# Hybrid encoder layer on one core: cross-attention scores of passes two to four from seven of eight block products, with the weights' block sums made in two side jobs

## The chip, the cores and the metric

The kernel runs on one core of a Trainium2 chip. Five engines matter here, and each works through its own list of instructions strictly in order: PE (matrix products, with its weight loads shown apart as PEld), DVE (vector work), ACT (scalar work and activations), POOL (small vector work, and the issuing of some DMAs), SP (the issuing of most DMAs). The metric is the device time of one execution in microseconds. Below, q0 to q3 are the four groups of 512 tokens in the setup's linears, and "pass 0 to 3" are the four passes of the later stage over the same groups; the title's "passes two to four" are passes 1, 2 and 3 by their number in the code.

## The reference, cut to what matters

```python
h = x + concat(dilated_attention(q, k, v), conformer_conv(a, g)) @ w_out   # q, k, v, a, g = rmsnorm(x) @ w_in
xq = (rmsnorm(h) @ w_xq).reshape(B, S, 4, 256)
xk = (rmsnorm(mem) @ w_xk).reshape(B, 256, 4, 256)
xv = (rmsnorm(mem) @ w_xv).reshape(B, 256, 4, 256)
sc = einsum('bshd,bmhd->bhsm', xq, xk) * 256 ** -0.5
h = h + (einsum('bhsm,bmhd->bshd', softmax(sc), xv)).reshape(B, S, D) @ w_xo
h = h + square(relu(rmsnorm(h) @ w_up)) @ w_down
return rmsnorm(h)                                   # S = 2048 tokens, D = 1024, w_up to 4096
```

## The kernel before

**Arithmetic.** Every fp32 product is made of three fp16 products, high by high, high by low and low by high (`mm3`, L374 to L376). A weight tile is loaded as fp32 and split into its high part by ACT (L361) and its low part by DVE (L362).

**The setup** (to about 500 us) folds the memory's keys into the scratch array `ascr`, so that the cross-attention's scores are one product of the token columns with a 1024 x 512 matrix for each of two pairs of heads, and its values into `bscr`. Then it makes the linears q, k, the conv's gate and input (`glu`: unit g, then unit a, for each of four column groups) and v, over all 2048 tokens. The raw weights of q lie in the slots q0 to q3 of the pool `wqk` (tiles `qksq`), those of k in q4 to q7. The part around 400 us runs: the last q tile (512 tokens by all of q's weights), the gate unit g3 (weights `ws_g30`), the input unit a3 (weights `ws_a30`), then v (`wv0`, `wv1`). Woven in between are the weights' bounds (`scan`: loads on SP, sums of squares into `sjunk` on ACT), the first token group's convolution (`conv0`, DVE), and `vscale`: for each of four column groups it squares the v weights (`vsq`, ACT, L760 on), sums them by eight thin matmuls into `vss` (PE, L767), and brings the square root's power of two by DVE and POOL to `vbc` (PE, L355), by which DVE scales the raw v weights (L798); ACT rounds them to `wv` (L800), POOL makes the low part (L801).

**The passes.** `post(p)` handles 512 tokens: the out projection (`resid_linear`, "o"; it leaves the residual `h` and, by ACT and DVE, the token columns `yh` and `yl` for the next product, L1531 and L1532), the scores (`xs`, L1772 to L1790), the softmax and its transposes, the product with `bscr` ("x"), and the MLP (up and down). While a pass runs, `weave` puts in the next pass's attention (`att`), its convolution (`conv`) and the sums of `prep`, so many steps of each to one of the pass.

**The scores before** are for each pass two pairs of heads x 8 groups of 128 columns of D x 4 groups of 128 tokens x 3 = 192 matmuls of 128x512. The weights come from `ascr` in four fp32 tiles a pair, split on ACT and DVE (`wpost`).

**Seven of eight.** Part of the MLP's up products are made already with seven instead of eight block products (`quad`, L1660 to L1714). Its weights' block sums are made by `prep` (L1536 to L1605) in earlier passes and stored to the scratch array `ust`, seven tiles of 512 KB for each group; its token columns come from `put_columns` (L1623 to L1649), which writes sums such as `T1`, `T4`, `B2`, `T32` instead of `yh` and `yl`. `prep` makes a group in two halves: two loads `pw0`, `pw1`, then four sums (`ps`, in place in `pw`) and four tiles `pt0` to `pt3`, each a high part by ACT and a low part by DVE, and a store of each.

**What sets the order.** A scheduler fixes each engine's list when the kernel is built, from the program's order, the steps that `weave` mixes and the constraints of `pinned` and `after`. A tile in a pool's slot waits for the last reader of the tile that had the slot before.

Of the kernel before, what the change touches and what calls it, by code (L numbers as in the profile page):

```python
# [10 lines left out]
F32 = mybir.dt.float32  # L11
# [10 lines left out]
P = 128  # L22
# [26 lines left out]
def hybrid_layer(ctx, tc, A, out):  # L49
# [70 lines left out]
    ust = [[dr.tile([P, 2 * 1024], F16, name=f"ust{fg}_{i}") for i in range(7)] for fg in range(8)]  # L120
# [26 lines left out]
    gxm = cst.tile([P, 24], F32, name="gxm")  # L147
# [5 lines left out]
    cst.tile([P, 56], F32, name="cpad")  # L153
# [101 lines left out]
    def bounds():  # L255
# [9 lines left out]
        with ExitStack() as st:  # L265
# [15 lines left out]
            TS(c[18], c[18], 16.0, None, op0=ALU.mult)  # L281
# [11 lines left out]
        with ExitStack() as st:  # L293
# [14 lines left out]
            TS(gxm[:, 16:24], gxm[:, 8:16], -1.0, None, op0=ALU.mult)  # L308
        yield
# [153 lines left out]


# [542 lines left out]
    vsc = vscale()  # L1007
    scn = pinned(chain(scan(), bounds()), "pe", "act")
    with ExitStack() as st:
        cu = pool("conv0", stack=st)  # L1010
        conv0 = pinned(conv_units(cu, 0, ahead=False), "dve")
        with ExitStack() as st2:
            lbk = pool("lin_k", stack=st2)
            weave(islice(steps, 2), (vsc, 0.4))
            weave(islice(steps, 32), (vsc, 0.4), (conv0, 0.78), (scn, 1.6))
            drain(vsc)
            next(steps)
        lbv = pool("lin_v", stack=st)
        weave(islice(steps, 3), (scn, 2))
        weave(islice(steps, 5), (conv0, 1.05), (scn, 2))  # L1020
# [3 lines left out]
        weave(steps, (conv0, 1.05), (scn, 2))  # L1024
        drain(conv0, scn)
# [347 lines left out]
    def flat(t):  # L1373
        return t.rearrange("p h a b -> p (h a b)")

# [133 lines left out]
    def resid_linear(load, rhs, korder, resid, hs, ssum, scale, gains, y, name, steps=False, wide=False, put=None):  # L1509
# [26 lines left out]
    def prep(fgs, q):  # L1536

        late = []

        def give(d, t):  # L1540
            late.append((d, t))

        def step():
            for d, t in late:
                dma(d, t, q)
            late.clear()

        def hi(o, i):
            ACT.activation(o, i, AF.Copy, scale=S_UP)

        def lo(o, i, h):
            DVE.scalar_tensor_tensor(o, i, S_UP, h, op0=ALU.mult, op1=ALU.subtract)

        for fg in fgs:
            for j in range(2):
                nm = f"{fg}{j}"
                raw = [ct0.tile([P, 8, P], F32, tag=f"ch{i}", name=f"pw{i}_{nm}") for i in range(2)]
                step()
                for i in range(2):
                    dma(raw[i], wcols(w_up, (4 * fg + 2 * i + j) * P), q)  # L1560
# [46 lines left out]
    def columns(p):  # L1607

        names = {"B11": 0, "T1": 1, "T4": 2}
        if p == 1:  # L1610
            names["B12"] = 7
# [567 lines left out]
```

## Time and profile before

| | |
|---|---|
| times of three runs (us) | 2649.49, 2649.41, 2641.41; median 2649.41 |
| the profiled execution's own time (us) | 2644.86 |
| its span in the profile (us) | 2643.0 |
| busy: PE, DVE, ACT, POOL | 2588.1 (98%), 1947.6 (74%), 1239.1 (47%), 307.3 (12%) us |
| score stages of passes 1, 2 and 3 (us from the span's start) | 1235.2 to 1290.6, 1747.0 to 1795.5, 2237.1 to 2281.3 |
| last q tile's matmuls end | 386.5 us |
| `ws_g30`'s last matmul starts; first v matmul | 397.0 us; 409.8 us |

Times in the profile are microseconds from the span's start unless marked ns. A row of groups by line gives line, engine, operation, output <- inputs, sizes and count, then busy time, mean ns of one, the idle time just before them and what ended most of it. A row of one tile gives shortest/mean/longest ns, then when the first and last began. A row of the timeline gives start, duration, engine, line, operation. In rows of windows the columns are the window, its length, each engine's busy time with its count of instructions, the granted clock of PE, the share of time that the DMA engines were busy, and GB/s.

### The profile page before, as it was taken

Reading aid. Unit: us, or ns where it says so; the run is one execution under the profiler, and the core shown is the slowest. Engines: PE = TensorE matmul, PEld = TensorE weight load, DVE = VectorE, ACT = ScalarE, POOL = GpSimd, SP = SyncE. Lnnn points to the kernel's source line nnn. Section 1 sums busy time; section 2 is a strip of 40 time slices with the busy share of each in tenths; the row PEclk is TensorE's granted clock in tenths of the full one; section 3 lists DMA queues with packets and bytes.
Section 4 is the critical chain, followed back from the end, with each engine's and each line's share of the span. In section 5 each row is a group of like instructions: output and inputs, shape, how many; then the busy total and the mean of one; then the engine's idle time right before and its main releaser. Section 6 shows DMA issues by size and latency. Waiting matters only on the chain.

```text
span 2643.0 us, 45573 instructions
## 1 busy us (share of the span) xinstructions
PE 2588.1 (98%) x17710; PEld 1650.8 (62%) x17710; DVE 1947.6 (74%) x3775; ACT 1239.1 (47%) x2194; POOL 307.3 (12%) x417
## 2 busy tenths in 40 slices
PE   8999999999999999999999999999999999999998
PEld 7844448777455555545576676555776664468886
DVE  5887756567667999775799986467899557675666
ACT  5737645376454345544553344255443234452323
POOL 1134101132100110110001111000110000000000
PEclk9999999999999999999999999999999999999999
DMA  8987977766634657785367677454686465345442
GB/s 263 300 266 221 284 233 258 194 177 189 186 98 139 193 175 244 219 271 162 108 213 218 200 240 238 165 162 132 216 264 192 145 203 167 100 133 170 156 138 78
DMA packets 401753, 509.51 MB, mean 193 GB/s; under 512 B 81181, under 2 KB 295121, under 8 KB 400768
## 3 DMA queue, kind: packets, MB, share of 16 engines
q1 hardware_dynamic: 380816, 446.35, 55.3%
q0 software_dynamic: 15536, 51.24, 6.0%
q10 hardware_dynamic: 5184, 9.01, 0.9%
q8 instruction: 139, 2.28, 0.4%
q14 instruction: 78, 0.64, 0.1%
HBM read 390.75 MB, written 115.75 MB: 192 GB/s over the span
## 4 chain that ended last, share of the span: by engine, by line
PE 77%; DVE 12%; DMA 6%; issue 2%; ACT 2%; SPq 0%; POOL 0%; DVEq 0%; POOLq 0%; ACTq 0%
PE dn L375 7%; PE dn L376 7%; PE dn L374 7%; PE up L376 6%; PE up L375 6%; PE up L374 6%; PE lin L376 3%; PE lin L374 3%; PE lin L375 3%; DVE cacc L391 3%; PE xs L375 2%; PE xs L376 2%; PE xs L374 2%; PE pt L1047 2%; PE o L374 2%
## 5 line engine op out<-in xcount | busy, mean ns | idle before, releaser
L391 DVE SCALAR_TENSOR_TENSOR cacc<-cu,cw,cacc 128x512 f32<-128x512 f32 x480 | 364.4, 765 | 5.5
L375 PE MATMUL dn<-hhl,ws_d 128*128 128x512 f16 x768 | 290.6, 379 | 1.4 <-DVE hhl L1878 0.8
L374 PE MATMUL dn<-hhh,ws_d 128*128 128x512 f16 x768 | 287.9, 379 | 3.7 <-ACT hhh L1655 2.3
L376 PE MATMUL dn<-hhh,ws_d 128*128 128x512 f16 x768 | 290.5, 379 | 0.0
L1040 DVE CUSTOM_DVE_ANT_0 sm<-s,mask,qks 128x256 f32<-128x256 f32 (+1 forms) x384 | 151.1, 433 | 31.6 <-PE s L1081 28.0
L1041 ACT ACTIVATE sm<-sm,o 128x256 f32<-128x256 f32 (+1 forms) x288 | 119.3, 455 | 110.9 <-DVE o L1040 110.3
L1051 DVE TENSOR_TENSOR pl<-pt,ph 128x512 f16<-128x512 f32 x160 | 109.7, 685 | 42.1 <-ACT ph L1050 41.7
L374 PEld LDWEIGHTS <-ws_t 128*128 128x128 f16 x1232 | 120.6, 98 | 18.2 <-DMA ws_t<-ust 1.8
L376 PEld LDWEIGHTS <-ws_d 128*128 128x128 f16 x768 | 75.1, 98 | 90.4 <-issue 2.0
L375 PEld LDWEIGHTS <-ws_t 128*128 128x128 f16 x1232 | 120.5, 98 | 17.5 <-issue 2.3
L1050 ACT CAST ph<-pt 128x512 f16<-128x512 f32 x160 | 91.4, 571 | 84.5 <-PE pt L1047 84.3
L376 PEld LDWEIGHTS <-ws_t 128*128 128x128 f16 x1232 | 120.5, 98 | 16.8 <-issue 1.1
L374 PEld LDWEIGHTS <-ws_d 128*128 128x128 f16 x768 | 75.1, 98 | 84.7 <-issue 2.5
L375 PEld LDWEIGHTS <-ws_d 128*128 128x128 f16 x768 | 75.4, 98 | 83.7 <-issue 1.6
L1904 DVE SCALAR_TENSOR_TENSOR h<-dn,bd,h 128x512 f32<-128x512 f32 x96 | 71.5, 746 | 74.0 <-PE dn L376 73.7
L1047 PE MATMUL pt<-ident,sm 128*128 128x128 f32 x640 | 98.2, 274 | 4.6 <-ACT sm L1041 2.9
L374 PE MATMUL up<-mh,ws_u 128*128 128x512 f16 x256 | 98.1, 383 | 2.1 <-DVE rl L1875 2.1
L1687 ACT ACTIVATE e<-e 128x512 f32<-128x512 f32 x88 | 55.2, 629 | 95.3 <-DVE e L1685 95.3
L376 PE MATMUL up<-mh,ws_u 128*128 128x512 f16 x256 | 98.1, 384 | 1.3 <-DVE ws_u L362 1.3
L375 PE MATMUL up<-ml,ws_u 128*128 128x512 f16 x256 | 98.1, 383 | 0.0
L374 PE MATMUL up<-T32h,ws_t 128*128 128x256 f16 x352 | 95.9, 273 | 2.1 <-DMA ws_t<-ust 2.1
L374 PE MATMUL o<-cath,ws_o 128*128 128x512 f16 x256 | 96.5, 379 | 0.9 <-ACT cath L1219 0.8
(560 smaller groups left out, 7751.3 us busy)
## 6 DMA issues: line engine op xcount, KB each, us to landing
ws_t<-ust SPq DMA_DIRECT2D x154, 512.0 KB
ws_d<-wst SPq DMA_DIRECT2D x80, 512.0 KB
ust<-pt POOLq DMA_DIRECT2D x36, 512.0 KB, 5.1
scan<-in_w_up_dram SPq DMA_DIRECT2D x32, 512.0 KB
scan<-in_w_down_dram SPq DMA_DIRECT2D x32, 512.0 KB
raw_o<-in_w_out_dram SPq DMA_DIRECT2D x32, 512.0 KB
raw_a<-ascr SPq DMA_DIRECT2D x32, 512.0 KB
raw_b<-bscr SPq DMA_DIRECT2D x32, 512.0 KB
```

The source lines that it names most:

```text
L374: PE.matmul(o, lh, rh, start=first, stop=False, skip_group_check=more)
L375: PE.matmul(o, lh, rl, start=False, stop=False, skip_group_check=more)
L376: last["pe"] = PE.matmul(o, ll, rh, start=False, stop=end, skip_group_check=more)
L391: DVE.scalar_tensor_tensor(acc, u[:, t:t + 512], cw[:, c, t:t + 1], acc, op0=ALU.mult, op1=ALU.add)
L1040: last["dve"] = DVE.tensor_tensor_reduce(dst, so, mask[:, 256 * m:256 * m + nk], SCORE, 3e38, ALU.add, ALU.min, mn)
L1041: last["act"] = ACT.activation(dst, dst, AF.Exp, bias=mn, scale=-1.0)
L1047: last["pe"] = PE.transpose(pt[:, j, :], sm[:, j, :], ident)
L1050: ACT.copy(ph, pt)
L1051: DVE.tensor_tensor(pl, pt, ph, op=ALU.subtract)
L1687: ACT.activation(e, e, AF.Square)
L1904: last["dve"] = DVE.scalar_tensor_tensor(hs[m], pt, K_DN, hs[m], op0=ALU.mult, op1=ALU.add)
```

## The change

Passes 1, 2 and 3 make each pair of heads' scores with seven block products instead of eight: a product is (256 tokens) x (512 columns of D) x (256 score columns), so 2 x 4 x 3 = 24 matmuls of 128x256, and a pass has 2 pairs x 7 x 24 = 336 of them. The weights' sums come from two new groups of `ust`, 8 and 9, one for each pair, with 14 loads of 512 KB a pass on SP in the place of eight fp32 loads and splits. The out projection's columns of these passes go through `put_columns`. The partial scores are kept in fp32 tiles on ACT, completed by DVE and pass through the softmax per 256 x 256 block. Pass 0 keeps the old scores.

`prep` makes the sums of both groups: group 8 in the setup, with its loads and stores issued by POOL and its four large tiles in the slots q0 to q3 of `wqk`; group 9 in pass 0, with loads and stores issued by SP and its tiles in the slots of pass 0's attention columns. Its scale S_A is computed by the new `side_scale` ahead of group 8.

```diff
+    def side_scale():
+        c = bd[:, 59:60]
+        with ExitStack() as st:
+            after(st, "pe", "dve")
+            pc = ps("c", "asum")
+            n = AS[1] - AS[0]
+            PE.matmul(pc[:, 0:n], onesq, acc2[:, AS[0]:AS[1]], start=True, stop=True)
+            DVE.tensor_reduce(c, pc[:, 0:n], axis=AX.X, op=ALU.add)
+            DVE.tensor_scalar(c, c, 4.0, None, op0=ALU.mult)
+        yield
+        pow2(S_A, I_A, None, 32768.0, "dve", of=c)
...
-    def prep(fgs, q):
+    def prep(fgs, q, alloc):
...
-                raw = [ct0.tile([P, 8, P], F32, tag=f"ch{i}", name=f"pw{i}_{nm}") for i in range(2)]
+                raw = [alloc(f"ch{i}", (P, 8, P), F32, f"pw{i}_{nm}") for i in range(2)]
                 step()
                 for i in range(2):
-                    dma(raw[i], wcols(w_up, (4 * fg + 2 * i + j) * P), q)
+                    if fg < 8:
+                        dma(raw[i], wcols(w_up, (4 * fg + 2 * i + j) * P), q)
+                    else:
+                        v = ascr[fg - 8].rearrange("p (h j k) n -> p h j k n", h=2, j=2)
+                        dma(raw[i].rearrange("p (h k c) m -> p h k (c m)", h=2, k=2),
+                            v[:, :, j, :, 256 * i:256 * i + 256], q)
...
+    def side_tile(tag, shape, dtype, name):
+        at = {"ch0": "q0", "ch1": "q1", "cl0": "q2", "cl1": "q3"}.get(tag)
+        return wqk.tile(list(shape), dtype, tag=at, name=name) if at else t2(name, dtype, shape)
+
+    side = pinned(chain(side_scale(), prep((8,), POOL, side_tile)), "dve", "act")
...
-            weave(islice(steps, 32), (vsc, 0.4), (conv0, 0.78), (scn, 1.6))
+            weave(islice(steps, 13), (vsc, 0.4), (conv0, 0.78), (scn, 1.6))
+            weave(islice(steps, 19), (vsc, 0.4), (conv0, 0.78), (scn, 1.6), (side, 1))
...
-        weave(islice(steps, 3), (scn, 2))
-        weave(islice(steps, 5), (conv0, 1.05), (scn, 2))
+        weave(islice(steps, 3), (scn, 2), (side, 1))
+        weave(islice(steps, 5), (conv0, 1.05), (scn, 2), (side, 1))
...
-        weave(steps, (conv0, 1.05), (scn, 2))
-        drain(conv0, scn)
+        weave(steps, (conv0, 1.05), (scn, 2), (side, 3))
+        drain(conv0, scn, side)
...
-        y = ytiles("y")
+        y = put = None
+        if p:
+            one, two_, side = columns(p, "s")
+            put = put_columns(one, two_, hs, 0, 24)
+        else:
+            y = ytiles("y")
...
+            def done(e, pt, i, z):
+                last["dve"] = DVE.tensor_tensor(e, e, pt, op=ALU.add)
+                soft_block(e, z)
+                late.append((pth, ptl, i, z, e))
...
+            prod(X, w11, "B11")
+            e1 = kept(X, "e1")
+            w2, w1 = pair(2)
+            prod(Z, w1, "T1")
+            e4 = kept(Z, "e4")
+            turn()
+            yield
+            prod(Y, w12, "B21")
+            done(e1, Y, 0, 0)
+            t = tile(6)
+            prod(X, w2, "T2", True)
...
+            if p:
+                for _ in side_quad(hp, pth, ptl):
...
-            weave(islice(main, 23 if p else 29), *sides)
+            if p:
+                weave(islice(main, 23), *sides)
+            else:
+                side = pinned(prep((9,), None, pass_tile), "dve", "act")
+                weave(islice(main, 2), *sides)
+                weave(islice(main, 27), *sides, (side, 0.8))
+                drain(side)
```

How the lists moved is shown at three places. In a row the number after a name's last underscore tells tiles apart. First ACT, from the high part of one of the last k and q stores to the weights of v. Before, the weights of a3 stood ahead of the gate's activations:

```order
L915 ACTIVATE qh_q33_4209<-lin_4184,qks_269 128x512
L230 ACTIVATE sjunk84_4139,acc2_266<-scan84_4138 128x1024
L58 DMA qscr_68<-qh_q33_4209 128x512
L230 ACTIVATE sjunk85_4143,acc2_266<-scan85_4142 128x1024
L361 ACTIVATE ws_a30_4232<-raw_a30_3858,wsc_262 128x1024
L743 ACTIVATE sig3_0_4265<-lin_4240,wsc_262 128x512
L743 ACTIVATE sig3_1_4296<-lin_4271,wsc_262 128x512
L230 ACTIVATE sjunk86_4182,acc2_266<-scan86_4181 128x1024
L800 CAST wv0_4306<-raw_v00_4037 128x8x128
```

The same engine in the changed kernel, from the second half of group 8 on:

```order
L500 ACTIVATE pt2_81_4009<-pw1_81_3865,bd_277 128x1024
L500 ACTIVATE pt0_81_3961<-pw0_81_3864,bd_277 128x1024
L852 ACTIVATE vsq31_3994<-vsq31_3994 128x512
L500 ACTIVATE pt3_81_4094<-pw0_81_3864,bd_277 128x512
L835 ACTIVATE sig3_0_4338<-lin_4313,wsc_276 128x512
L835 ACTIVATE sig3_1_4369<-lin_4344,wsc_276 128x512
L230 ACTIVATE sjunk85_4255,acc2_280<-scan85_4254 128x1024
L500 ACTIVATE pt1_81_4091<-pw0_81_3864,bd_277 128x512
L500 ACTIVATE pt1_81_4091<-ps1_81_3963,bd_277 128x512
L892 CAST wv0_4379<-raw_v00_4109 128x8x128
L230 ACTIVATE sjunk86_4290,acc2_280<-scan86_4289 128x1024
L378 ACTIVATE ws_a30_4305<-raw_a30_3908,wsc_276 128x1024
```

The square `vsq31` of the last v column group now stands behind `pt2_81` and `pt0_81`, and the weights `ws_a30` behind all of `pt*_81`, the first rounding of `wv0` and a scan. Second, PE where g3 ends. Before, with a part of `vbc` between g3 and a3:

```order
L376 LDWEIGHTS ws_g30_4033
L376 MATMUL lin_4271<-xh3_1_1491,ws_g30_4033 128x512
L355 MATMUL vbc00_4307<-ident_241,vmul_255 128x128
L374 LDWEIGHTS ws_a30_4232
L374 MATMUL lin_4317<-xh0_0_664,ws_a30_4232 128x512
L375 LDWEIGHTS ws_a30_4232
L375 MATMUL lin_4317<-xl0_0_665,ws_a30_4232 128x512
```

In the changed kernel:

```order
L393 LDWEIGHTS ws_g30_4105
L393 MATMUL lin_4344<-xh3_1_1505,ws_g30_4105 128x512
L859 MATMUL vss3_4233<-ones_260,vsq30_3993 128x1 x4
L859 MATMUL vss3_4233<-ones_260,vsq31_3994 128x1 x4
L203 MATMUL p2_4296<-wsc_276,onesq_272 128x1
L372 MATMUL vbc00_4380<-ident_255,vmul_269 128x128
L372 MATMUL vbc01_4385<-ident_255,vmul_269 128x128
L391 LDWEIGHTS ws_a30_4305
L391 MATMUL lin_4390<-xh0_0_678,ws_a30_4305 128x512
```

The sums `vss3` moved from ahead of the last q tile to behind g3, with `p2` and both `vbc` behind them. Third, POOL in the changed kernel, with the semaphores that each waits for, from the first half's stores to the low part of `wv0`:

```order
L58 DMA ust8_0_238<-pt0_80_3628 128x2048 [waits DVE_49]
L58 DMA ust8_4_242<-pt2_80_3670 128x2048 [waits DVE_49]
L58 DMA pw1_81_3865<-ascr_253 128x4x256 [waits DMASW1_49]
L58 DMA ust8_6_244<-pt3_80_3761 256x1x512 [waits DVE_49]
L58 DMA pw0_81_3864<-ascr_253 128x4x256 [waits DMASW0_49,DVE_49]
L58 DMA ust8_2_240<-pt1_80_3758 128x2048 [waits DVE_49]
L58 DMA ust8_5_243<-pt2_81_4009 128x2048 [waits DVE_49]
L58 DMA ust8_1_239<-pt0_81_3961 128x2048 [waits DVE_49]
L862 TENSOR_TENSOR vs3_4242<-vs3_4242,mhalf_264 128x1 [waits DVE_49,Pool_49]
L208 TENSOR_TENSOR p2s_281<-p2s_281,mhalf_264 128x1 [waits DVE_49]
L58 DMA ust8_6_244<-pt3_81_4094 256x1x512 [waits DMASW2_49,DVE_49]
L893 TENSOR_TENSOR wv0_4379<-raw_v00_4109,wv0_4379 128x8x128 [waits Activation_49]
```

Before, this stretch of POOL held no DMA: there the two powers `vs3` and `p2s` are followed by clearings of six small tiles and then by the low part of `wv0`. In the changed kernel the power for `vs3` is queued behind the stores of both halves. The first loads of group 8, `pw0_80` and `pw1_80`, wait there for PE, the last reader of the q weights in their slots.

More of the change, by code (lines that the diff above doesn't have):

```diff
@@ L146, in hybrid_layer @@
     bd = cst.tile([P, 64], F32, name="bd")
[L147 removed]
+    gxm = cst.tile([P, 32], F32, name="gxm")
     vcat = cst.tile([P, 4], F32, name="vcat")
@@ L1793, in post @@
         if p:
-            one, two_, src = columns(p)
-            put = put_columns(one, two_, hs)
+            one, two_, src = columns(p, "")
+            put = put_columns(one, two_, hs, 8, 16)
             y = None
```

223 lines of the change are left out of this document (149 added, 74 removed).

## The prediction

> **What bounds the kernel now.** I read the page first, its busy row, the chain of waits and the granted clock.
>
> ```profile
> PE 2588.1 (98%) x17710; PEld 1650.8 (62%) x17710; DVE 1947.6 (74%) x3775; ACT 1239.1 (47%) x2194; POOL 307.3 (12%) x417
> PE 77%; DVE 12%; DMA 6%; issue 2%; ACT 2%; SPq 0%; POOL 0%; DVEq 0%; POOLq 0%; ACTq 0%
> ```
>
> PE is the limit: 98% busy, at a full granted clock nearly everywhere. So a matmul less is time gained one for one, and a wait of PE is time lost one for one; work of other engines costs only where PE ends up waiting for it. Next I read the windows of the three score stages that change, and of the setup where group 8 is put. (Columns: window, length, busy PE, PEld, DVE, ACT, POOL with counts, granted clock, DMA share, GB/s.)
>
> ```profile
> 1235.20:1290.60 55.40, 55.07 (x327) 29.30 (x325) 35.03 (x82) 27.26 (x56) 3.97 (x4) 1.00 0.46 133
> 2237.10:2281.30 44.20, 44.14 (x217) 21.47 (x216) 32.02 (x55) 21.04 (x37) 1.01 (x1) 1.00 0.34 110
> 382.00:397.00 15.00, 15.00 (x73) 6.95 (x72) 6.64 (x13) 6.03 (x10) 0.78 (x7) 1.00 0.68 216
> 397.00:419.00 22.00, 20.64 (x141) 13.80 (x140) 9.35 (x11) 14.45 (x24) 7.84 (x5) 1.00 0.75 255
> ```
>
> In the score stages PE is all but full, and DVE has 32.0 of 44.2 us, ACT 21.0, so both have room. In the setup PE is full to 397.0 and loses 1.4 us after it; there DVE and ACT are far from full, so it is the order and the transfers that decide, not their work.
>
> **The matmuls.** A matmul's shown duration overlaps the next one's, so I take the spacing of starts in long undisturbed rows: 512 wide in pass 3's scores (rows 11 starts apart), 256 wide in the MLP's seven-of-eight product (16 apart).
>
> ```profile
> 2244.62 0.38 PE L375 MATMUL xs<-ws_a,yh 128*128 128x512 f16 x1
> ...
> 2247.00 0.38 PE L375 MATMUL xs<-ws_a,yh 128*128 128x512 f16 x1
> 2454.21 0.27 PE L374 MATMUL up<-T32h,ws_t 128*128 128x256 f16 x1
> ...
> 2455.96 0.27 PE L375 MATMUL up<-T32l,ws_t 128*128 128x256 f16 x1
> ```
>
> (2247.00 − 2244.62)/11 = 0.2164 us and (2455.96 − 2454.21)/16 = 0.1094 us. Before: 192 x 0.2164 = 41.5 us a pass; after: 336 x 0.1094 = 36.8. That is 4.8 us gained a pass, **−14.3 us** for three. The 256-wide row is the same form of instruction, with weights from the same array at the same rate, as the new scores would issue.
>
> One rule would turn this round. The Trainium skill ("TensorE: Matmul & The Clock Gate", section on the back-to-back issue gap) gives sustained spacings of about 81 ns at N=128 and 131 ns at N=512; between them my estimate at 256 is 98 ns. By it the scores would go from 192 x 131 = 25.1 us to 336 x 98 = 32.9 us, a loss of 7.7 us a pass. Here the trace disagrees: its fp16 matmuls are spaced 216 and 109 ns, nearly in proportion to their width, and the measurement decides.
>
> **What group 8 does to the setup.** This is the term that decides the sign. Group 8's first loads go into slots that hold the q weights until the last q tile has read them. In the timeline and by tile:
>
> ```profile
> 382.59 0.38 PE L376 MATMUL lin<-xh,qksq 128*128 128x512 f16 x1
> ...
> L376 PE MATMUL lin<-xh,qksq x128: 377/379/380, 235.1 to 386.5; 128*128 128x512 f16 x128
> L376 PE MATMUL lin<-xh,ws_g x64: 376/379/631, 141.4 to 397.0; 128*128 128x512 f16 x64
> L361 ACT ACTIVATE ws_a<-raw_a,wsc x1: 1132/1132/1132, 389.7 to 389.7; 128x1024 f16<-128x1024 f32 x1
> L767 PE MATMUL vss<-ones,vsq x64: 167/250/251, 255.4 to 376.2; 128*128 128x1 f32 x64
> 409.83 0.27 PE L375 MATMUL v<-wv,xh 128*128 128x256 f16 x1 [1.36 <-POOL wv L801]
> ```
>
> The matmul at 382.59 is the last reader of the slot of `pw0_80`, so this load starts at about 383.0, and `pw1_80`'s some 1.2 us later. Before, the weights of a3 were split at 389.7, long before PE needed them (g3 ends just after 397.0), and `vss3` ran at 376. In the changed order ACT's high part of `ws_a30` stands behind all tiles of group 8's second half, and `vsq31`, for which PE's `vss3` waits right behind g3, behind `pt2_81` and `pt0_81`. So PE stands still from 397.0 until the second half of group 8 is through on ACT. What that takes comes from the same job for the MLP's groups, which exists already:
>
> ```profile
> L58 POOL DMA_DIRECT2D pw<-in_w_up_dram x24: 887/917/1035, 1243.8 to 1958.6; - x24
> DMA to landing us min/median/max: 4.8/7.1/10.0
> L58 POOL DMA_DIRECT2D ust<-pt x48: 537/555/716, 1356.7 to 1998.0; - x48
> DMA to landing us min/median/max: 2.9/5.4/9.2
> ...
> ust<-pt POOLq DMA_DIRECT2D x36, 512.0 KB, 5.1
> L1549 ACT ACTIVATE pt<-pw,bd 128x1024 f16<-128x1024 f32 x32 | 36.4, 1142 | 28.9 <-DMA pw<-in_w_up_dram 23.4 <-DVE pw L1569 5.2
> L1549 ACT ACTIVATE pt<-pw,bd 128x512 f16<-128x512 f32 x32 | 22.8, 713 | 23.3 <-DMA ust<-pt 13.7 <-DVE pw L1579 6.5 <-DVE pw L1574 2.9
> L1552 DVE SCALAR_TENSOR_TENSOR pt<-pw,bd,pt 128x1024 f16<-128x1024 f32 x32 | 40.6, 1273 | 0.3 <-ACT pt L1549 0.3
> L1552 DVE SCALAR_TENSOR_TENSOR pt<-pw,bd,pt 128x512 f16<-128x512 f32 x32 | 23.8, 744 | 1.7 <-ACT pt L1549 1.7
> L1568 DVE TENSOR_TENSOR ps<-pw 128x512 f32<-128x512 f32 x16 | 10.9, 683 | 0.0
> L1579 DVE TENSOR_TENSOR pw<-pw 128x512 f32<-128x512 f32 x16 | 11.7, 731 | 0.0
> L230 ACT ACTIVATE sjunk<-scan x18: 1046/1056/1058, 359.7 to 417.1; 128x1024 bf16<-128x1024 f32 x18
> L798 DVE TENSOR_TENSOR raw_v<-raw_v,vbc x4: 1212/1218/1222, 397.5 to 413.5; 128x1024 f32<-128x1024 f32 x4
> L800 ACT CAST wv<-raw_v x4: 1027/1040/1046, 399.0 to 414.7; 128x1024 f16<-128x1024 f32 x4
> ```
>
> For a landing I choose 6.0 us for loads and 5.1 for stores. The first is the middle of shortest and median, the second the page's median for the stores of 512 KB, which are POOL's own in the passes; the DMA engines' share here, 0.68 to 0.75, speaks against the shortest. Walk, in us of the profiled execution:
>
> - First half. `pw0_80` lands at 389.0, `pw1_80` at 390.2. Sum s1 to 390.9, low part of pt0 to 392.2, three sums in place to 394.2, low part of pt2 to 395.5, of pt3 to 396.2. pt0's store is issued at 392.2 and lands at 397.3. pt1 takes pt0's slot, so ACT makes it only then, 397.3 to 398.7, and DVE its low parts to about 399.
> - Second half. The loads reuse the first half's slots: `pw1_81` leaves behind pt0's and pt2's stores at 396.1 and lands at 402.1; `pw0_81` waits for DVE's last reading of its slot at 398.8 and lands at **404.8**. A sum to 405.5, ACT's pt2_81 to 406.6, pt0_81 to 407.8, vsq31 to 408.4. PE's `vss3` ends at 409.3; DVE, which has low parts and sums to 410.6 ahead, and POOL bring the two vbc; DVE scales raw_v00 to 413.6.
> - ACT meanwhile needs pt0_81's store (issued 409.2, landed 414.3) for pt1_81, done at 415.7; then wv0's rounding 416.8, a scan 418.0, and `ws_a30`'s high part **419.2**.
>
> PE thus stands from 397.0 to 419.2. As g3's last matmul takes 0.2 us of this by its spacing, I count 22 us, **+22 us**. Behind it nothing further is late: v's weights are ready before a3's 13 us of matmuls end, which also takes away the wait of 1.36 us, **−1.4**. POOL's powers and stores are in the walk. Bounds: with the shortest landings, 4.8 and 2.9, the same walk resumes at 414.9 (stall 18); with the medians, 7.1 and 5.4, at 422.5 (25.5); with the longest, 10.0 and 9.2, at 435.9 (39). Below 18 only if the slots come free earlier.
>
> For landings one rule bears on it: the Trainium skill ("DMA: Bandwidth & Descriptors", section on the anatomy of one DMA, SWDGE path) has 2.0 us + bytes/436e3, by my estimate 3.2 us for 512 KB. By it the stall would be some 15 us and the sum about +2. The trace's shortest load is 4.8 and its median 7.1, so it disagrees, and I keep the measured ones.
>
> After a stall PE's clock can fall. The row after a wait of 2.0 us later in the setup:
>
> ```profile
> 541.59 0.44 PE L1047 MATMUL pt<-ident,sm 128*128 128x128 f32 x2 [1.97 <-ACT sm L1041]
> ...
> 540.00:544.00 4.00, 1.93 (x17) 0.79 1.03 357
> 544.00:548.00 4.00, 4.00 (x36) 0.79 0.79 208
> ```
>
> The windows 540 to 548 have a granted 0.79 (here PE busy, clock, DMA share and GB/s last): 8 x 0.21 = **+1.7** us.
>
> **Group 9 in pass 0.** Its loads go into slots of the attention columns that the out projection reads to its end, in a stage where DVE has 9 to 12 of 15 us:
>
> ```profile
> 705.00:720.00 15.00, 15.00 (x71) 6.81 (x70) 11.83 (x16) 7.10 (x10) 0.00 (x0) 1.00 0.65 207
> 720.00:735.00 15.00, 14.65 (x75) 7.16 (x73) 9.25 (x19) 6.58 (x9) 1.05 (x1) 1.00 0.63 187
> ```
>
> Each group is some 15 us of DVE (per half four sums 2.8, two low parts 2.5, three halves 2.2) and 9 of ACT. Over the 100 us through which it is woven this fits into the idle fifth to third of DVE. What is queued behind it: the first low part, waiting for a load whose slot comes free 2.6 us before the projection ends, holds up the last `yl`, which the scores need some 15 us later by the order of the scores' eight k-groups. So 0; at worst a long landing and the sums behind it, 4 us. I take **+1**.
>
> **Around the new scores.** DVE gains `put_columns` and the additions of `done` and loses the splits and the `yl`:
>
> ```profile
> L1643 DVE TENSOR_TENSOR B2l<-yv,B2h 128x512 f16<-128x512 f32 x12 | 8.2, 684 | 0.0
> L1683 DVE TENSOR_TENSOR e<-e,up 128x512 f32<-128x512 f32 x88 | 59.4, 682 | 47.5 <-ACT e L1679 32.5 <-PE up L376 14.8
> L362 DVE SCALAR_TENSOR_TENSOR ws_a<-raw_a,bd,ws_a 128x1024 f16<-128x1024 f32 x32 | 40.9, 1280 | 16.0 <-ACT ws_a L361 16.0
> L1532 DVE SCALAR_TENSOR_TENSOR yl<-h,gxm,yh 128x512 f16<-128x512 f32 x32 | 23.2, 745 | 0.4 <-ACT yh L1531 0.4
> ```
>
> By the program: 8 additions x 0.68 = 5.5 and column sums of about 17 (24 of the 512-wide and 8 of the half-wide form, at 0.68 and somewhat less), against 8 x 1.28 + 8 x 0.745 = 16.2: +6.6 us in a stage with 12 us free. ACT loses 8 x 1.15 and gains 8 copies at about 0.6 and some halves, within 3 us either way. The tightest place is pass 3, where sums for the MLP stand between: by the order and these rows DVE has the last B2 column 4.7 us after the projection's end and the last T32 column 14.5 us after, and PE has 54 x 0.109 = 5.9 and 141 x 0.109 = 15.4 us of products before each. So the columns are just covered; with the cover gone it costs 1 to 2 us a pass. Against that stand the waits for the transposes' low parts of 0.5 to 1.0 us a stage, four in all, −2.9, which smaller blocks may or may not take away. Six more loads a pass go from SP at the up product's own rate. I take **0**, between −2.9 and +6.
>
> **Sum.** −14.3 + 22 − 1.4 + 1.7 + 1 + 0 = **+9.0 us** on the profiled execution's 2644.86 (span 2643.0 and 1.86 around it): about 2654. The median of the three runs, 2649.41, is 4.55 above it and one run is 3.45 below, so on the median's scale it is 2658. I name **2657**.
>
> **Rivals.** *Short landings* (0.24): loads and stores take 4.8 and 2.9; stall 18, the sum +5, 2650 to 2654. For it: POOL's queue is otherwise empty there. Against: a DMA share of 0.75. *Long landings* (0.12): the transfers collide with the scan's and v's loads; stall 26 to 39, sum +13 to +26, 2658 to 2675. *The block is covered* (0.07): that is the other side. The mechanism is ACT's `ws_a30` being ready within 7.8 us of g3's end (404.8): then the stall is below 7.8 and the sum at most −5; with no stall it is −14.3 − 1.4 + 1 = about −14, 2631 to 2636. Its price is decided by when the q weights' slots come free; the matmul at 382.59 speaks against it, since ready at 404.8 would need two rounds of load, sums and store in 22 us, where two shortest loads and two shortest stores alone take 15.4. *The delay is absorbed* (0.07): PE's waits in the attention after the setup sum to 9.4 us from 380 to 720,
>
> ```profile
> PE pt L1047 <- ACT sm L1041: 2.9, 3, 2.0
> ```
>
> of which the longest kind is shown (sum, count, longest). If DVE and the DMAs run ahead during the stall, some go: sum 0 to +5. Against: the waits are for work that starts after PE's own. *The skill's spacing* from above (below 0.01, within the forecast's remainder): the sum near +46.
>
> **The numbers.** Forecast +9 (stall 20 to 26): 0.50. 0.3% is 7.9 us and about what measurement tells from no change. Slower: long landings 0.12, and of the forecast's cases, which spread +5 to +14, some 0.44: 0.56. Same: the rest of the forecast 0.06, short landings 0.24, absorbed 0.07: 0.37. Faster 0.07. The range for eight in ten, 2644 to 2671, spans stalls of about 10 to 35; it leaves out the covered block and the longest landings.
>
> **What would show it.** In the changed profile: PE idle for some 22 us near 397, released by ACT's `ws_a`, with `vss` just ahead; `pw0_81` landing near 405; 256-wide `xs` rows at 0.109 us and score stages 4 to 5 us shorter; no new wait over 1 us at their start or in pass 0. I am wrong if PE's gap is below 8 us (then it is faster), if the gap shows but the stages do not shrink, or if a fourth place with a wait of several us appears.

## The result, and the profile after

| | before | changed |
|---|---|---|
| first runs: median of four (us) | 2647.25 | 2671.78 (2664.67 to 2674.71) |
| ratio | | 1.0092, 95% interval 1.0065 to 1.0119 |
| once more, beside other runs on one chip: median (us) | 2640.67 | 2673.97; ratio 1.0123 (1.0107 to 1.0138) |
| the profiled execution's span (us) | 2643.0 | 2672.9 |

The kernel became 24.5 us slower in the first runs and 33.3 in the second; the two profiled executions differ by 29.9. Forecast were +9.0 on the profiled scale and 2657 in all: the sign was right, the size was not, and the time lies above the range's end of 2671.

First the page's busy row of the changed kernel. PE is busy 1.5 us less than before although it runs 434 matmuls more (432 of them in the scores, each half as wide), and the span is 29.9 us longer: the loss is waiting, and a clock that falls with it.

```profile
PE 2586.6 (97%) x18144; PEld 1697.7 (64%) x18144; DVE 1987.4 (74%) x3904; ACT 1270.5 (48%) x2262; POOL 318.2 (12%) x430
```

Where it went is read by stages. The table gives each stage's length in us in one profiled execution, taken from the first and last matmuls of the tiles that bound it (last q tile, last v tile, first o and last x of each pass). Rows that name several passes add their stages. The two profiles of the changed kernel differ by up to 3.4 us in a stage, so a difference of 3 us or less is near what one profile can tell.

| stage | before | changed | changed, again | forecast |
|---|---|---|---|---|
| last q tile to the end of v | 145.1 | 172.4 | 174.5 | +22.3 |
| pass 0, o to x | 149.0 | 162.7 | 161.8 | +1 |
| pass 0, MLP | 375.5 | 375.3 | 374.7 | 0 |
| passes 1 to 3, o to x | 426.2 | 414.8 | 417.7 | −14.3 |
| passes 1 and 2, MLP | 707.4 | 710.8 | 707.4 | 0 |

**The setup's gap** is the one that was forecast, and it ends within 0.5 us of the walk. PE's timeline around it in the changed kernel (the idle time before an instruction, and what ended it, in brackets):

```profile
395.19 0.38 PE L393 MATMUL lin<-xh,ws_g 128*128 128x512 f16 x1
399.92 1.87 PE L859 MATMUL vss<-ones,vsq 128*128 128x1 f32 x8 [4.36 <-ACT vsq L852]
410.13 1.87 PE L859 MATMUL vss<-ones,vsq 128*128 128x1 f32 x8 [8.34 <-ACT vsq L852]
...
415.43 0.48 PE L372 MATMUL vbc<-ident,vmul 128*128 128x128 f32 x1 [1.38 <-DVE p2s L209]
419.73 0.61 PE L391 MATMUL lin<-xh,ws_a 128*128 128x512 f16 x1 [3.83 <-ACT ws_a L378]
```

g3's last matmul starts at 395.2, and a3's first at 419.7, where the walk had 419.2. Here one sees how to read a chain of small waits: PE's list holds `vss`, `p`, `vbc` and `ws_a` one behind the other, each released late by ACT or DVE, and the idle times in brackets are pieces of one delay. That it came out so closely is partly luck. The landings were 7.1 us at the median for the loads (6.0 taken) and 4.2 for the stores (5.1 taken), errors that cancel: `vss` ends at 412.0 where the walk had 409.3, but ACT, which in the walk waits until 414.3 for a store before it makes `pt1_81`, comes to it only at 415.3 and then waits no longer. The rows of the tiles `pw` and `ust` from 370 to 470 us:

```profile
DMA to landing us min/median/max: 5.5/7.1/7.7
```

```profile
DMA to landing us min/median/max: 2.6/4.2/7.1
```

**Pass 0** is the surprise. The windows of the changed kernel there (length, busy PE, PEld, DVE, ACT, POOL with counts, clock, DMA share, GB/s), and PE's waits from 720 to 870 us, with those of the kernel before from 700 to 830 us below the dots (sum, count, longest):

```profile
745.00:765.00 20.00, 20.00 (x102) 9.95 (x101) 14.88 (x25) 11.69 (x15) 1.05 (x1) 1.00 0.64 210
765.00:785.00 20.00, 16.51 (x89) 8.38 (x88) 13.76 (x38) 10.12 (x25) 0.00 (x0) 0.91 0.62 181
785.00:805.00 20.00, 18.30 (x118) 10.05 (x116) 16.30 (x35) 12.65 (x26) 0.00 (x0) 1.00 0.39 130
805.00:825.00 20.00, 16.77 (x100) 9.86 (x98) 9.84 (x28) 8.36 (x18) 0.20 (x1) 0.83 0.33 79
```

```profile
PE xs L391 <- ACT xp L1791: 3.0, 1, 3.0
PE pt L1146 <- DVE ptl L1805: 2.4, 1, 2.4
PE s L1180 <- DVE o L1139: 1.7, 1, 1.7
...
PE pt L1047 <- DVE ptl L1766: 0.4, 1, 0.4
PE xs L374 <- DVE h L1527: 0.3, 1, 0.3
```

DVE has 4 to 10 us free in each window of 20, as the prediction had counted, and yet PE waits for results of DVE and ACT. What stands ahead of them shows in DVE's timeline before the 3.0 us wait:

```profile
765.98 0.75 DVE L503 SCALAR_TENSOR_TENSOR pt<-pw,bd,pt 128x512 f16<-128x512 f32 x1
766.65 0.75 DVE L503 SCALAR_TENSOR_TENSOR pt<-ps,bd,pt 128x512 f16<-128x512 f32 x1
767.31 0.75 DVE L503 SCALAR_TENSOR_TENSOR pt<-pw,bd,pt 128x512 f16<-128x512 f32 x1
767.97 1.28 DVE L379 SCALAR_TENSOR_TENSOR ws_a<-raw_a,bd,ws_a 128x1024 f16<-128x1024 f32 x1
769.17 1.88 DVE L1788 TENSOR_REDUCE xmx<-xs 128x2 f32<-128x512 f32 x3
```

Three half-wide low parts of group 9, 2.0 us together, run right ahead of `ws_a` and the maxima `xmx`, without which ACT can't empty the scores' banks (where PE's products land); PE then waits from 769.4 on for such a bank.

**The scores.** The windows of the three score stages, and two rows of pass 3, 8 matmuls apart:

```profile
1277.90:1324.60 46.70, 44.70 (x441) 40.46 (x440) 32.65 (x85) 25.25 (x58) 1.91 (x2) 1.00 0.46 152
1784.20:1830.30 46.10, 44.57 (x443) 40.38 (x441) 33.24 (x88) 25.32 (x59) 1.92 (x2) 1.00 0.53 163
2270.20:2314.10 43.90, 40.77 (x366) 35.61 (x365) 37.21 (x73) 25.10 (x50) 1.12 (x1) 1.00 0.53 173
```

```profile
2274.76 0.27 PE L391 MATMUL xs<-ws_s,T1h3s 128*128 128x256 f16 x1
...
2275.64 0.27 PE L393 MATMUL xs<-ws_s,T1l3s 128*128 128x256 f16 x1
```

The spacing is (2275.64 − 2274.76)/8 = 0.110 us, as forecast. But PE is no longer full in these stages; its waits of 1.5 us or more there, one of each pass:

```profile
PE xs L391 <- DVE h L1624: 1.9, 1, 1.9
...
PE nps L1584 <- DVE ssumo L1575: 1.5, 1, 1.5
...
PE xs L391 <- ACT T4h3s L1680: 1.9, 1, 1.9
```

### The profile page after: what moved, and what is told of

Same layout as the page of the kernel before. It is cut to its first block, busy times and chain, and to the rows that moved or that the text cites. A ratio compares the mean times of both kernels' runs of the same rounds, so it can differ in the third digit from the quotient of the medians.

```text
span 2672.9 us, 46731 instructions
## 1 busy us (share of the span) xinstructions
PE 2586.6 (97%) x18144; PEld 1697.7 (64%) x18144; DVE 1987.4 (74%) x3904; ACT 1270.5 (48%) x2262; POOL 318.2 (12%) x430
## 4 chain that ended last, share of the span: by engine, by line
PE 51%; DVE 10%; DMA 6%; issue 2%; ACT 1%; POOL 0%; SPq 0%; DVEq 0%; POOLq 0%; ACTq 0%
PE dn L392 7%; PE dn L393 7%; PE dn L391 7%; PE up L393 5%; PE up L391 5%; PE up L392 5%; DVE cacc L408 2%; PE x L391 2%; PE x L393 2%; PE x L392 2%; DMA res<-xscr 2%; DMA pw<-in_w_up_dram 2%; PE xs L391 1%; PE xs L393 1%; PE xs L392 1%
## 5 line engine op out<-in xcount | busy, mean ns | idle before, releaser
L500 ACT ACTIVATE pt<-pw,bd 128x1024 f16<-128x1024 f32 (+1 forms) x80 | 73.9, 927 | 63.6 <-DMA pw<-in_w_up_dram 22.3
L364 POOL TENSOR_TENSOR nr<-st_v,mhalf 128x4 f32<-128x4 f32 (+1 forms) x15 | 15.1, 1009 | 704.6 <-DVE st_v L360 704.6
```

Source lines behind the costliest of these rows:

```text
L500: ACT.activation(o, i, AF.Copy, scale=S_UP if fg < 8 else S_A)
```

## The experiments

Each is a variant of the changed kernel. Its time is a median, its ratio is to the kernel before on the same chip, with a 95% interval.

| | what | us | ratio |
|---|---|---|---|
| 1 | sums made, scores as before | 2681.91 | 1.0152 (1.0130 to 1.0173) |
| 2 | group 8 in v | 2659.24 | 1.0065 (1.0047 to 1.0083) |
| 3 | group 9 on POOL's queue | 2668.92 | 1.0099 (1.0072 to 1.0126) |
| 4 | both groups in v | 2666.15 | 1.0093 (1.0070 to 1.0115) |
| 5 | group 9 in pass 0's MLP | 2666.96 | 1.0100 (1.0078 to 1.0121) |
| 6 | group 8 earlier in v | 2663.91 | 1.0077 (1.0057 to 1.0098) |
| 7 | 5 and 6 together | 2655.24 | 1.0050 (1.0034 to 1.0066) |
| 8 | the changed kernel again | 2673.97 | 1.0123 (1.0107 to 1.0138) |
| 9 | passes 2 and 3 alone, sums in pass 1 | 2668.15 | 1.0105 (1.0089 to 1.0120) |
| 10 | pass 3 alone, sums in pass 2 | 2645.80 | 1.0019 (1.0010 to 1.0028) |
| 11 | as 10, sums ten steps later | 2644.59 | 1.0006 (0.9997 to 1.0015) |
| 12 | group 9's transfers without its sums | 2663.23 | 1.0081 (1.0065 to 1.0096) |

Stage lengths of their profiles, read as above (us):

| | q to v | pass 0 o to x | pass 0 MLP | passes 1 to 3 o to x | MLP of pass 1 | MLP of pass 2 |
|---|---|---|---|---|---|---|
| before | 145.1 | 149.0 | 375.5 | 426.2 | 360.3 | 347.1 |
| 1 | 174.1 | 163.7 | 375.3 | 424.8 | 359.1 | 347.3 |
| 2 | 160.6 | 161.7 | 375.6 | 416.5 | 359.2 | 347.1 |
| 3 | 173.1 | 157.5 | 375.4 | 416.0 | 358.6 | 347.1 |
| 4 | 181.2 | 151.0 | 374.3 | 414.9 | 360.3 | 349.9 |
| 5 | 174.3 | 149.7 | 384.5 | 410.5 | 357.5 | 348.1 |
| 6 | 162.2 | 164.2 | 375.2 | 416.5 | 361.0 | 349.9 |
| 7 | 162.5 | 149.8 | 383.7 | 411.9 | 358.2 | 347.6 |
| 9 | 147.0 | 149.6 | 375.0 | 421.5 | 387.3 | 348.4 |
| 10 | 148.8 | 149.2 | 375.4 | 421.0 | 357.5 | 354.8 |
| 11 | 147.9 | 150.1 | 374.3 | 420.9 | 359.1 | 352.8 |
| 12 | 172.1 | 149.8 | 375.6 | 420.6 | 358.2 | 348.2 |

### 1. The sums alone

```diff
-        if p:
+        if False:
             one, two_, side = columns(p, "s")
...
-            if p:
+            if False:
                 for _ in side_quad(hp, pth, ptl):
```

> Both groups' sums are made as in the changed kernel, but the scores of all passes are computed as before (192 matmuls of 128x512 a pass), so the sums are made and not used. Theory: the two side jobs cost about 25 us in the setup and 13 us in pass 0, and the seven-of-eight scores give back 11 to 14 us; so this kernel should be 34 to 42 us slower than before, with the changed kernel's gap near 397 us, and with score stages of passes 1 to 3 as long as before. Rival: part of the loss comes with the new scores (their six more loads a pass, their column work); then this kernel is at most 25 us slower than before.

39.2 us slower than before: the theory's case. The setup's 29.0 us and pass 0's 14.7 stand without the new scores, and the score stages are 1.4 us shorter than before. So the new scores themselves give 7 to 10 us: 424.8 here against 414.8 and 417.7 in the changed kernel's two profiles.

### 2 and 6. Group 8 in v

```diff
-            weave(islice(steps, 19), (vsc, 0.4), (conv0, 0.78), (scn, 1.6), (side, 1))
+            weave(islice(steps, 19), (vsc, 0.4), (conv0, 0.78), (scn, 1.6))
...
-        weave(islice(steps, 3), (scn, 2), (side, 1))
-        weave(islice(steps, 5), (conv0, 1.05), (scn, 2), (side, 1))
+        weave(islice(steps, 3), (scn, 2))
+        weave(islice(steps, 5), (conv0, 1.05), (scn, 2), (side, 0.8))
...
-        weave(steps, (conv0, 1.05), (scn, 2), (side, 3))
+        weave(steps, (conv0, 1.05), (scn, 2), (side, 1.5))
```

> Group 8 is woven into the v linear alone, behind the weights of a3 and v; everything else as in the changed kernel. Theory (the place in the lists of ACT, DVE and PE costs, not the work): a3's matmuls start right behind g3's, near 397 us, the 25 us are gone but for at most 6 us of new waits in v, and the time is 4 us below to 6 us above before. Rival (the work costs: 15 us of DVE, 9 of ACT and 4 MB of transfers crowd the setup wherever they stand): it stays 15 us or more above before.

By its number the rival came in: 16.5 us above before, where it had 15 or more. But a3 ends 1.6 us earlier than before (before: 407.9), so the gap at 397 is gone, as the theory had it; what the theory missed is that v ends 13.8 us late. The two largest waits in v and the first attention, 400 to 570 us; in the kernel before the first is 0.4 and the second the same 2.5, and its clock is 1.00 from 500 to 520 us, here 0.83:

```profile
PE s L1180 <- DVE o L1139: 8.5, 3, 4.7
PE pt L1146 <- ACT sm L1140: 2.5, 2, 2.0
```

And from the rows of the tile `mask`:

```profile
L58 SPq DMA_DIRECT2D mask<-in_masks_dram x1: 475/475/475, 491.9 to 491.9; - x1
```

The attention's mask is loaded at 491.9 (454.3 before), after the group's last store, which POOL issues at 486.1, and on SP right behind a store of `u` that waits 4.6 us for DVE. I took the group's end for the cause. The sixth experiment lets group 8 begin earlier, its edit being the removal from the first line above and 1.6 for the rate 1 in the line of five steps:

> As the second experiment, but group 8 starts some steps earlier, with its first high part behind v's 4th tile of tokens and its last ahead of the 17th; group 9 as in the changed kernel. There the first attention's mask load started only at 491.9 us, behind the group's last store. Theory (v's loss of 14 us came from the group's end lying too late, so that the attention's tiles, which follow in the same memory, were loaded late): with the group done some 30 us earlier the loss in v falls to 5 us or less and the whole to 2 to 9 us above before. Rival (ACT's waits for the group's transfers, ahead of the weights' bounds and of v's outputs, cost in v by themselves): the loss in v stays 10 us or more, the whole at 12 us or more.

The rival came in, 23.2 us above before: the mask is loaded at 471.2, nothing waits for it, and v still ends 15.7 us late. Now PE waits elsewhere:

```profile
PE sums L251 <- ACT sjunk L230: 5.7, 1, 5.7
PE s L1180 <- DVE o L1139: 3.1, 2, 2.7
```

The scan's squares, from which the weights' bounds are summed on PE, stand behind the group's tiles on ACT, which waits there 4.9 us for a load and 1.8 for a store of the group. My first story of the mask explained one wait of the second experiment and not the stage.

### 3. Group 9 on POOL's queue

```diff
-                side = pinned(prep((9,), None, pass_tile), "dve", "act")
+                side = pinned(prep((9,), POOL, pass_tile), "dve", "act")
```

> Group 9's loads and stores in pass 0 are issued by POOL and no longer by SP; everything else as in the changed kernel. Theory A (SP's queue: the stores of group 9 wait there for DVE's low parts, and the residual, score weight and key loads stand behind them): pass 0's extra 13 us fall to 5 or less, the whole to 15 us or so above before. Theory B (the order on DVE and ACT: scales, maxima and attention's parts stand behind the group's tiles): pass 0 still costs 10 us or more, and the whole is 21 us or more above before.

Pass 0 falls from 162.7 to 157.5 us, and the whole stays 26.2 us above before: theory B by the whole, between the two by the stage, where 5.2 us go and 8.5 stay. Two of PE's waits of this kernel in the stage, and its windows at the stage's start and around the first of these waits:

```profile
PE pt L1146 <- DVE ptl L1805: 2.4, 1, 2.4
...
PE xs L391 <- ACT xp L1791: 0.9, 1, 0.9
```

```profile
695.70:715.70 20.00, 17.02 (x131) 9.53 (x128) 9.80 (x30) 8.41 (x17) 1.63 (x3) 0.91 0.83 185
...
795.70:815.70 20.00, 15.22 (x108) 9.13 (x106) 16.31 (x43) 12.49 (x31) 1.27 (x3) 1.00 0.31 103
815.70:835.70 20.00, 18.94 (x114) 9.70 (x115) 14.73 (x26) 12.62 (x22) 1.23 (x2) 1.00 0.52 151
```

The wait for the scores' banks is 0.9 us instead of 3.0, which is 2.1 us. The wait for `ptl` is 2.4 us in both kernels, but the clock fell behind it in the changed kernel (0.83 above) and not here. The only low clock of this stage is at its start, 20 x 0.09 = 1.8 us, where the changed kernel has 5.2 by its windows; that is the other 3.4. So the larger part of the 5.2 us is clock, and beyond the 2.1 us this run shows no price of SP's queue.

### 4. Both groups in v

```diff
-    side = pinned(chain(side_scale(), prep((8,), POOL, side_tile)), "dve", "act")
+    side = pinned(two_groups(), "dve", "act")
...
+        a, b = prep((8,), POOL, side_tile(0)), prep((9,), POOL, side_tile(4))
+        for _ in range(3):
+            next(a)
+            yield
+        for _ in b:
+            yield
+            next(a, None)
+            yield
```

> Both groups are woven into the v linear, one behind the other by a few steps, on POOL's queue, with the slots of the q weights for group 8 and those of the k weights for group 9; pass 0 has no side job, as before. Theory: the 13 us of pass 0 go away, the 25 us of the setup too but for waits where v's 17th tile of tokens stands behind the last low parts (up to 10 us); the three score stages still give 11 us: in all between 12 us faster and 3 us slower than before. Rival (the work costs wherever it is put): 10 us or more slower than before.

The rival came in, 23.4 us above before. Pass 0 is back at 151.0, within 2 us of before, but the setup's stage takes 36 us more than before. ACT's waits of this kernel, 400 to 570 us, show what a side job does to an engine that is mostly free:

```profile
ACT pt L500 <- DMA ust<-pt: 13.7, 4, 8.4
ACT pt L500 <- DMA pw<-ascr: 12.0, 2, 7.5
```

ACT stands 26 us for the groups' own transfers. What PE needs of ACT stands behind: PE waits 9.6 us for the conv gate's activation, here the longest of its waits, and 7.2 for the scan's squares.

```profile
PE lin L391 <- ACT sig L835: 9.6, 1, 9.6
```

### 5 and 7. Group 9 in the MLP of pass 0

```diff
-    preps = {0: (0, 1), 1: (3, 5, 6, 7), 2: (4, 2)}
+    preps = {0: (9, 0, 1), 1: (3, 5, 6, 7), 2: (4, 2)}
...
-            sides.append((prepping[p], 1.2 if p else 0.9))
+            sides.append((prepping[p], 1.2 if p else 1.35))
```

> Group 9 is taken out of pass 0's projection and score stages and put in front of the MLP's groups 0 and 1 in pass 0's MLP stage (same queue, same slots, 1.35 steps to one of the pass where it was 0.9); group 8 stays as in the changed kernel. Theory (the place costs: in the projection and score stages ACT's and DVE's lists hold the group's waiting tiles ahead of what PE needs next): pass 0 from its projection's start to its x product's end takes 149 to 152 us as before, where the changed kernel takes 162.6, its MLP stage grows by at most 4 us, and the whole is 10 to 16 us above before. Rival (the group's work and traffic cost PE about 13 us wherever they stand, since DVE is 97% busy in most of the MLP stage): 21 us or more above before.

The rival came in, 26.3 us above before (the profiled execution is the fastest of the four, with a span 17.3 us above before). Pass 0's first part is as before (149.7), but its MLP grows by 9.0 us. PE's waits of this kernel from 840 to 1232 us; in the kernel before the first stood at 2.1 and the second at 0.8:

```profile
PE up L391 <- DVE rl L2009: 5.7, 1, 5.7
PE dn L392 <- DVE hhl L2012: 2.6, 3, 1.2
PE pt L1146 <- DVE pl L1150: 2.1, 1, 2.1
```

With group 8 early in v besides:

> Both moves together: group 8 early in v, group 9 in pass 0's MLP stage. Theory: setup's loss 0 to 5, pass 0's 0 to 4, scores -10: 10 us faster to 1 us slower than before. Rival (the work costs wherever it is): 8 us or more slower.

14.6 us slower: both moves add up (setup 17 us, MLP 8, scores −14). The rival came in.

### 8. The changed kernel again

> The changed kernel as it is, once more beside these runs, for a comparison on the same chip: both theories expect 20 to 28 us above before.

33.3 us above before, more than both had; the stages repeat within 3.5 us.

### 9, 10 and 11. The sums in later passes

The ninth has `if p >= 2` for `if p` at the scores, no side job ahead of pass 1, and `1: (3, 5, 6, 7, 8, 9)` in `preps`; the tenth `p >= 3` and `2: (4, 2, 8, 9)`; the eleventh puts twelve empty steps between:

```diff
+            todo = prep(preps.get(p, ()), POOL if p else None, pass_tile)
+            if p == 2:
+                todo = chain(todo, (None for _ in range(12)), prep((8, 9), POOL, pass_tile))
```

> Seven of eight in passes 2 and 3 alone; pass 1 scores as before. No side job in the setup or in pass 0: groups 8 and 9 are made behind groups 3, 5, 6 and 7 in pass 1's MLP stage (POOL's queue), whose last 120 us have DVE busy 25, 25 and 18 of 40 us in the kernel before. Theory (only where the sums are made decides; two passes of scores give 6 to 7 us): setup, pass 0 and pass 1's scores within 1 us of before, pass 1's MLP stage 0 to 4 us longer, passes 2 and 3 give 3 to 4 us each: 2 to 7 us faster than before. Rival (the sums cost 8 us and more a group wherever they are): 8 us or more slower.

The rival came in: 26.4 us slower, and pass 1's MLP 27 us longer. Of the two passes' scores pass 3 gives 4.5 us and pass 2 nothing (145.8 for 145.0). The last halves of the groups were not done when the stage's end came and were drained there, ahead of the last residual's squares:

```profile
PE nps L1583 <- DVE ssumf L1574: 13.3, 1, 13.3
```

It is the setup's gap over again, in another pass; the run tells little of a group's cost where there is room.

> Seven of eight in pass 3 alone; groups 8 and 9 are made behind groups 4 and 2 in pass 2's MLP stage, whose last 147 us have 65 us of DVE free and no wait of PE. Theory: the sums are hidden there, pass 3's scores give 3 to 4 us, the whole 2 to 4 us faster than before. Rival (the sums cost PE time wherever they are): slower than before by 4 us or more.

4.1 us slower, at the edge of the rival's case. Pass 3 gives 4.2 us (130.6 for 134.8), pass 2's MLP takes 7.7. The window from 2000 to 2040 us shows why free time is no measure: in this kernel (first row) DVE is busy for less of it than in the kernel before (second row), 32.42 us for 38.16, and yet PE waits.

```profile
2000.00:2040.00 40.00, 37.52 (x251) 23.01 (x249) 32.42 (x55) 7.95 (x14) 6.45 (x9) 1.00 0.79 257
2000.00:2040.00 40.00, 40.00 (x286) 26.39 (x285) 38.16 (x64) 7.51 (x15) 1.38 (x3) 1.00 0.61 188
```

The two largest of PE's waits in its MLP stage:

```profile
PE up L391 <- ACT e L1712: 3.2, 1, 3.2
PE dn L392 <- DVE hhl L1689: 2.0, 2, 1.4
```

> As the tenth experiment, but groups 8 and 9 start some ten steps later in pass 2's MLP stage, where in the kernel before DVE has 14 and 24 of 40 us; there the tenth had waits of PE of 3.2, 1.35 and four of 0.7 to 0.9 us between 2028 and 2084 us, where the kernel before has none. Theory (a group costs where DVE's list is near full, by its waiting tiles; with half of DVE free it costs nothing): pass 2's MLP stage within 1 us of before, pass 3 gives 3 to 4 us, the whole 2 to 4 us faster than before. Rival (it costs PE 4 us a group wherever it stands): 3 us or more slower.

No difference from before that could be measured, and neither case quite: pass 3 gives 4.3, pass 2's MLP still takes 5.7, with DVE busy 29 of 40 us where PE waits 3.6 us for it. So the theory that half of DVE free costs nothing isn't borne out, and why these two groups still cost isn't shown. This is the best of the variants; none beats the kernel before.

### 12. Group 9's transfers without its sums

```diff
+                if fg == 9:
+                    x = alloc("cl0", (P, 2, 8, P), F16, f"pt0_{nm}")
+                    POOL.memset(flat(x), 0.0009765625)
...
+                    give(ust[fg][j], flat(x))
...
+                    give(ust[fg][4 + j], flat(x))
...
+                    continue
```

> As the changed kernel, but group 9 in pass 0 makes no sums: its four loads go to the same slots and are not read, its eight stores write a constant tile that POOL fills, on the same queue; the scores of the second pair of heads in passes 1 to 3 then have constant weights. Theory (ACT's and DVE's lists cost, with the group's tiles ahead of the maxima and exponentials and halves that PE needs): pass 0 from its projection's start to its x product's end falls from 162.7 us to 149 to 152, as before, and the whole to 10 us or more below the changed kernel. Rival (its loads and stores cost, in the queue and the memory): pass 0 stays above 157 us.

In this kernel the second pair's scores have constant weights, so it is for timing alone. Pass 0 is at 149.8 us, as before the change, and the whole is 10.7 us below the eighth run: the theory's case. PE's waits from 720 to 850 us are these alone:

```profile
PE o L391 <- ACT cath L1335: 0.8, 1, 0.8
PE ptx L1819 <- DVE ptl L1822: 0.3, 1, 0.3
```

So four loads and eight stores on SP in that place cost PE nothing; the 13 us come with the sums: their work on ACT and DVE, their places there, and what waits for them. One thing changed with the sums: the stores wait for POOL's constant and no longer for DVE's low parts, so that the keys, queries and weights behind them on SP aren't held up. Whether that hold-up costs anything by itself, no run shows.

## Why the prediction was right in sign and wrong in size

- **The matmuls, −14.3: right** (−14.4 by its own spacings). Spacing of 0.110 us against 0.1094. By stages passes 1 to 3 gave 11.4 and 8.5 us; the difference is booked under the waits around the new scores, below.
- **Group 8 in the setup, +22, with −1.4 and +1.7: the mechanism, the place and the end of the gap as forecast** (419.7 for 419.2). The stage took 27.3 us more instead of 22.3. The setup ran 1.7 us earlier up to the gap (last q tile's end 385.2 for 386.9), and the gap's end did not, so that it was some 24 us long and not 22; a3, at a low clock, took 13.6 us from its first matmul to its end (433.3), for 10.6 before (397.3 to 407.9), where +1.7 was counted; and the −1.4 of v's wait was taken back by a wait of 1.7 in the first attention. The prediction's 13 us for a3 before were misread: the v matmul at 409.8 is the first behind the wait of 1.36, the first of all starts at 407.9. The sign is no luck: these 27.3 us outweigh what the scores give, without any of pass 0.
- **Group 9 in pass 0, +1: the step that failed.** The prediction said that 15 us of DVE "fits into the idle fifth to third", followed one instruction behind it (the last `yl`) and bounded the rest by 4 us. It measured 13.7 and 12.8. Some 8.5 us of it were waits and 5.2 the clock behind them, which this term counted with nothing. The twelfth experiment took the sums away and the loss went with them. It is 12.7 of the 20.9 us by which the forecast on the profiled scale fell short. What failed is the reasoning from free time: the question is not whether DVE has 15 us to spare in 100, but what stands behind each of the group's instructions while it waits or runs. I asked this for group 8, and it gave the right place; for group 9 I asked it of one row and let the shares answer for the rest. The maxima and the transposes' low parts, for which PE then waited 3.0 and 2.4 us, were in the lists. "No new wait over 1 us in pass 0" was one of the prediction's own signs, and it failed.
- **Around the new scores, 0 with bounds −2.9 and +6: on the wrong half,** 2.9 and 5.8 us of loss by the stages. New waits came for the residual `h` in pass 1 (1.9), for the squares' sum in pass 2 (1.5) and for a column, `T4h`, in pass 3 (1.9); the last is the cover of which I had written that it just holds.
- **The rivals.** Short and long landings: between, as taken. The covered block and the absorbed delay did not come: the gap shows in full, and from a3's end to v's end it takes 124.4 us in both kernels. The rival with the other spacing did not come either (0.110 us). I gave no rival to group 9's cost, and the range's end at 2671 was set by the setup's landings alone; the time lay beyond it by less than 1 us at first and by 3 in the second set.
- The sum with measured stages: 27.3 + 13.7 − 11.4 + 3.4 (the MLP stages, 0 when run again) − 3.1 (all else, the last q tile's end 1.7 us earlier among it) = 29.9.

## What to carry to other kernels

In these runs a block of work that waits for its own transfers cost by its place in the lists of in-order engines more than by its busy time: go through each engine it touches and name what the critical engine needs from behind it, in every place where it stands and not only in the worst. Here a group of some 15 us of DVE and 9 of ACT cost PE about 3 us at the least (two groups, 5.7, in the eleventh, near what one profile can tell) and 29 at the most in the places tried, and two of them undid a saving of 8 to 16 us. A saving that needs a side job should be weighed first by the side job alone.

## What was not expected of the hardware

Some waits cost more than their length, since PE's clock falls with them. In the changed kernel the windows over the gap and behind it (columns as above):

```profile
395.60:419.60 24.00, 5.27 (x20) 4.43 (x20) 13.77 (x25) 11.65 (x18) 8.84 (x11) 0.55 0.61 200
419.60:423.00 3.40, 3.27 (x10) 1.44 (x11) 2.17 (x3) 3.34 (x7) 2.54 (x3) 0.50 0.72 215
423.00:433.40 10.40, 10.40 (x45) 4.55 (x44) 0.70 (x2) 2.17 (x4) 0.75 (x1) 0.89 1.05 376
```

3.4 x 0.50 + 10.4 x 0.11 = 2.8 us are lost behind the gap, where the prediction had 1.7 from a wait of 2 us. The same is seen after a wait of 3.0 us, but only 1 us after PE had started again:

```profile
772.90 0.38 PE L393 MATMUL xs<-ws_a,yl 128*128 128x512 f16 x1
773.12 0.38 PE L391 MATMUL xs<-ws_a,yh 128*128 128x512 f16 x1
...
774.41 0.63 PE L392 MATMUL xs<-ws_a,yh 128*128 128x512 f16 x1
774.84 0.63 PE L393 MATMUL xs<-ws_a,yl 128*128 128x512 f16 x1
```

From 773.6 on the matmuls are spaced 0.43 us and not 0.22. Not every wait does it, and the length alone doesn't decide: after pass 3's wait of 1.9 us near 2286 us the windows have a full clock to 2296, after the kernel before's wait of 2.0 us near 541 the prediction's rows have 0.79, and the same wait of 2.4 us for `ptl` is followed by 0.83 in the changed kernel and by 1.00 in the third experiment. Of pass 0's loss of 13.7 us, by the windows shown for it, 20 x 0.09 + 20 x 0.17 = 5.2 us are low clock and the rest waits.

The Trainium skill ("TensorE: Matmul & The Clock Gate", the part on the HAM clock gate) says that the clock is halved after an idle window of about 3.4 us, and that this window runs freely and does not start anew with a kernel. The granted 0.50 and the delay of 1 us agree with a window of that kind, and the two outcomes of the same wait would fit it; but here a wait of 3.0 us, shorter than the window, was enough.
